# A short-convolution layer on one core: adaLN's weight loads on GpSimd's queue, paced by the other weights' splits

## The chip, the core and the metric

The kernel runs on one core of a Trainium2 chip. The metric is device time in microseconds (us), smaller is better. TensorE (PE in the profile) multiplies, VectorE (DVE), ScalarE (ACT) and GpSimd (POOL) compute beside it, and SyncE (SP) only starts DMA transfers. Each engine has a queue of instructions that it works through in order, and an instruction waits on semaphores for what it needs. A transfer is started by an instruction on some engine's queue, which waits there for its buffer to be free, and then runs on 16 DMA engines that all queues share.

## The reference

One layer of a decoder trunk (DEPTH is 1, so only the short-convolution mixer is used), for a sequence of 256 and a width of 2048, in float32:

```python
h = rmsnorm(x, norm_g[0])
mod = jnp.einsum('bd,df->bf', jax.nn.silu(c), ada_w) + ada_b     # adaLN: (2048) x (2048, 6144)
shift, scale, gate = jnp.split(mod, 3, axis=-1)
h = h * (1.0 + scale) + shift
proj = jnp.einsum('bsd,de->bse', h, w_in)                        # (256, 2048) x (2048, 16384)
b_gate, c_gate, v, g = jnp.split(proj, 4, axis=-1)
u = causal_depthwise_conv(c_gate * v, conv_w)
y = jnp.einsum('bse,ed->bsd', b_gate * u * silu(g), w_out)       # (256, 4096) x (4096, 2048)
out = rmsnorm(x + gate * y, final_g)
```

The weights are read once: `w_in` is 128 MB, `w_out` 32 MB, and adaLN's `ada_w` 48 MB, of which shift and scale take 32 MB and gate 16 MB. Shift and scale are needed before anything of `w_in` can be multiplied, row block by row block: row block k of h (128 of the 2048 rows, k from 0 to 15) needs 128 sums of shift and 128 of scale.

## The kernel before

**Float32 products by halves.** Each float32 weight tile `raw` is split into a rounded high part `hi` (a cast on ScalarE, line 324) and a low part `lo` (raw minus hi on VectorE, line 325), and so is h (`hT`). A product is three matmuls: hi by hi, hi by lo, lo by hi (line 417 to 419). `split` (lines 320 to 326) does this for one weight tile. The tiles `raw`, `hi` and `lo` have three buffers each. So the load of weight tile n waits for the low part of tile n-3, and the splits of tile n wait for TensorE to finish with tile n-3. The splits are counted here in the order in which the program makes them: 0 and 1 are in the front, 2 to 81 in the first main stage.

**The front** (lines 183 to 358) loads x, the vectors and the first 4 MB of adaLN for row blocks 0 and 1 (`first_ada`), sums these on VectorE and, in its last part, on TensorE (`sum0`, line 337; the call at line 351 is the last one), and makes row blocks 0 and 1 of `hT`. Its instructions are held in the order of the program.

**The first main stage** (mm_s, lines 444 to 502) works on half of `w_in`'s columns, in 16 sets (4 chunks by 4 quarters) of 512 columns. Since row blocks of h become ready only as adaLN's sums are done, each set is taken in several parts, first for the row blocks 0 and 1, later for more; what a part has summed is kept in `acc` and put back into the accumulator (`seed`). `part` (line 444) loads the weights in tiles of up to four row blocks (512 KB for two, 1 MB for four), splits each and multiplies.

**adaLN behind the front.** Row blocks 2 to 15 come in seven groups of two. A group is eight pieces (`ada_piece`, line 378): a piece loads, by two DMAs of 256 KB, two blocks of `ada_w`'s rows for shift and scale into a tile `at` (four buffers; the loads stand at line 388, on SP's queue), and sums them into `gv` by two VectorE operations of 512 elements (`ada_sums`, lines 394 to 401). After the eighth piece `ada_done` (line 403) adds up the partitions: TensorE transposes `gv` (`tp_g`, line 408), ScalarE sums the rows (line 410), and `modulate` (line 300) makes two row blocks of `hT`.

**What sets the order.** `plan` (line 52) is a planner with fixed costs: it lists parts and pieces in one order, in which a piece is put in wherever its load does not make the next weights late. The program is written down in this order, but a scheduler then orders each engine's queue by its own account of when each instruction can start; `later(300)` (line 168) makes an instruction 300 places less urgent, and `behind` and `add_manual_dep` with `after` are orders on one engine without a wait. So a load that needs only a free buffer can be put far ahead of its place in the plan. The planner's order puts the pieces ahead of the weights of these splits:

| row blocks | splits that the eight pieces stand ahead of | first needed by the weights of |
|---|---|---|
| 2, 3 | 4, 5, 7, 8, 9, 10, 12, 13 | 14 |
| 4, 5 | 14, 15, 16, 16, 17, 17, 19, 20 | 22 |
| 6, 7 | 21, 23, 23, 24, 24, 25, 26, 26 | 28 |
| 8, 9 | 27, 29, 29, 29, 31, 31, 33, 33 | 35 |
| 10, 11 | 34, 34, 36, 36, 38, 38, 38, 40 | 43 |
| 12, 13 | 40, 42, 42, 42, 44, 44, 46, 46 | 49 |
| 14, 15 | 46, 48, 48, 48, 50, 50, 50, 52 | 55 |

Splits 2 to 13 and 17 to 21 are of two row blocks, and so are some later ones (28, 30, 32 and others); most of the others are of four.

**Behind it** come the second half of `w_in` (mm_b, lines 545 to 581), with the loads and sums of adaLN's gate among it (`gate_piece`, line 520, and `gate_sums`, line 529: 32 loads of 512 KB into buffers of the same tag `at`), and then `w_out` (mm_o, lines 586 to 681).

Of the kernel before, what the change touches and what calls it, by code (L numbers as in the profile page):

```python
# [8 lines left out]
F32 = mybir.dt.float32  # L9
F32R = mybir.dt.float32r  # L10
AF = mybir.ActivationFunctionType
ALU = mybir.AluOpType

P = 128
# [3 lines left out]
KT = D // P  # L18
# [99 lines left out]
def short_conv_layer(ctx: ExitStack, tc: tile.TileContext, x, c, norm_g, ada_w, ada_b, w_in, conv_w, w_out, final_g, out):  # L118
    nc = tc.nc
# [19 lines left out]
    def raw_tile(name):  # L139
        return wpool.tile([P, SLOT], F32, tag="raw", name=name, bufs=3)  # L140

    after = mybir.DependencyInfo(mybir.DependencyClass.NoSync, mybir.DependencyReason.DATA)

    @contextmanager
    def in_order():
# [11 lines left out]
    @contextmanager  # L157
    def behind(last):

        traced = nc.cur_bb.bb.instructions  # L160
        n = len(traced)
        yield
        for ins in list(traced[n:]):
            if ins.engine in last:
                tc.add_manual_dep(ins, last[ins.engine], after, reason="behind")

    @contextmanager
    def later(n):

        now = tc.cur_priority  # L170
        tc.cur_priority = now + n
        yield
        tc.cur_priority = now
# [13 lines left out]
    GIVE = 300  # L187
# [12 lines left out]
    adas = ada_w[0].rearrange("(k p) (s f) -> p k s f", p=P, s=3)  # L200
# [18 lines left out]
    ones = const.tile([P, P], F32, tag="ones", name="ones")  # L219
# [38 lines left out]
    for t in range(TT):  # L258
        for dh in range(2):
# [3 lines left out]
            else:  # L263
                nc.vector.scalar_tensor_tensor(
                    out=junk[:, t], in0=xt[t][dh], scalar=1.0, in1=xt[t][dh], op0=ALU.mult, op1=ALU.mult,
# [54 lines left out]
    def split(raw, n, lo_tag="lo"):  # L320

        hi = wpool.tile([P, SLOT], F32R, tag="hi", name="hi", bufs=3)
        lo = wpool.tile([P, SLOT], F32R, tag=lo_tag, name="lo", bufs=3)
        nc.scalar.copy(hi[:, :n], raw[:, :n])  # L324
        nc.vector.tensor_tensor(out=lo[:, :n], in0=raw[:, :n], in1=hi[:, :n].bitcast(F32), op=ALU.subtract)  # L325
        return hi, lo


# [2 lines left out]
    gv0 = adap.tile([P, 2, 2 * P], F32, tag="gv", name="gv0")[:, :, 0 : NK0 * P]  # L331
    turn_x(0, 4)

    def sum0(k, rows, col):

        for o in range(2 * NK0):
            nc.tensor.matmul(
                sums0[:, o : o + 1], rows[:, o // NK0, (o % NK0) * P : (o % NK0 + 1) * P], col,
                start=k == ON_PE[0] and o == 0, stop=k is None, skip_group_check=True,
            )  # L340

    for k in range(KT):
        c_k = silu_c[:, k : k + 1]
# [4 lines left out]
            nc.vector.tensor_scalar_mul(gv0, first_ada[k], c_k)  # L348
        else:
            nc.vector.scalar_tensor_tensor(out=gv0, in0=first_ada[k], scalar=c_k, in1=gv0, op0=ALU.mult, op1=ALU.add)  # L350
    sum0(None, gv0, ones[:, 0:1])
    pieces0 = [split(raw0[:, 0 : CT * P], CT * P)]
    modulate(0, NK0, (sums0[:, 0:NK0], sums0[:, NK0 : 2 * NK0]))
    idle(IDLE[-1])
# [20 lines left out]
    acc = {}  # L375
    sums = {}

    def ada_piece(k0, nk, piece):
        w = nk * P
        kk = ASLOT // (2 * w)  # L380
        if piece == 0:
            sums[k0] = adap.tile([P, 2, 2 * P], F32, tag="gv", name="gv")
        gv = sums[k0][:, :, 0:w]
        j = piece * kk
        at = adap.tile([P, ASLOT], F32, tag="at", name="at", bufs=4)
        at4 = at.rearrange("p (k s f) -> p k s f", k=kk, s=2)
        for s in range(2):
            nc.sync.dma_start(at4[:, :, s, :], adas[:, j : j + kk, s, k0 * P : k0 * P + w])  # L388
        with later(GIVE):
            ada_sums(j, kk, at4, gv)  # L390
        if j + kk == KT:
            ada_done(k0, nk, gv)

    def ada_sums(j, kk, at4, gv):
        for i in range(kk):
            c_k = silu_c[:, j + i : j + i + 1]
            if j + i == 0:
                with behind(ended):
                    nc.vector.tensor_scalar_mul(gv, at4[:, i], c_k)
            else:  # L400
                nc.vector.scalar_tensor_tensor(out=gv, in0=at4[:, i], scalar=c_k, in1=gv, op0=ALU.mult, op1=ALU.add)  # L401

    def ada_done(k0, nk, gv):

        tp = psum.tile([P, 4, P], F32, tag="sm", name="tp_g", bufs=2)
        gs = const.tile([P, 4], F32, tag="gs", name="gs", bufs=2)
        for o in range(2 * nk):
            nc.tensor.transpose(tp[:, o, :], gv[:, o // nk, (o % nk) * P : (o % nk + 1) * P], ident)  # L408
        for o in range(2 * nk):
            nc.scalar.activation(tp[:, o, :], tp[:, o, :], AF.Copy, accum_out=gs[:, o : o + 1])  # L410
        modulate(k0, nk, (gs[:, 0:nk], gs[:, nk : 2 * nk]))
# [32 lines left out]
    def part(ch, q, k0, k1, seed):  # L444


        col = q * E + ch * CT * P
        step = SLOT // (CT * P)
        first = k0
        bank = psum.tile([P, CT, T], F32, tag="mm", name="mm_s")  # L450
        if seed:
            nc.scalar.copy(bank, acc[ch, q])
        if pieces0:
            for k in range(NK0):
                chunk_products(bank, *pieces0[k], 0, k, k0, k1, late=True)
            pieces0.clear()
            k0 = NK0
        for s0 in range(k0, k1, step):
            sk = min(step, k1 - s0)
            n = sk * CT * P  # L460
            raw = raw_tile("raw_s")
            nc.sync.dma_start(
                raw[:, :n].rearrange("p (k f) -> p k f", k=sk),
                w_in[0, s0 * P : (s0 + sk) * P, col : col + CT * P].rearrange("(k p) f -> p k f", p=P),
            )
            hi, lo = split(raw, n)
            for i in range(sk):
                chunk_products(bank, hi, lo, i * CT * P, s0 + i, k0, k1, seed)
        keep(ch, q, first, bank, seed)
# [57 lines left out]
            gate_sums(dc, j, at3)  # L527

    def gate_sums(dc, j, at3):
        nc.sync.dma_start(at3, adas[:, j : j + 2, 2, dc * 512 : (dc + 1) * 512])  # L530
        if j == 0:
            gacc[0] = adap.tile([P, 512], F32, tag="gv", name="gacc")
        ga = gacc[0]
        for i in range(2):
            s = silu_c[:, j + i : j + i + 1]
            if j + i == 0:
                nc.vector.tensor_scalar_mul(ga, at3[:, i, :], s)
            else:
                nc.vector.scalar_tensor_tensor(out=ga, in0=at3[:, i, :], scalar=s, in1=ga, op0=ALU.mult, op1=ALU.add)
        if j + 2 == KT:  # L540
            ps = psum.tile([P, 512], F32, tag="sm", name="ps_gate", bufs=2)
            nc.tensor.matmul(ps, ones, ga, start=True, stop=True)  # L542
            nc.vector.tensor_tensor(out=gate(dc), in0=ps, in1=gate(dc), op=ALU.add)
# [3 lines left out]
    for ct in range(NS, NCT, 2):  # L547
        for q in QUARTERS:
            bank = psum.tile([P, CT, T], F32, tag="mm", name="mm_b")[:, 0:2]
            col = q * E + ct * P  # L550
            for kp in range(0, KT, KP):
                raw = raw_tile("raw")
# [4 lines left out]
                hi, lo = split(raw, SLOT)  # L557
# [67 lines left out]
    for dc in range(4):  # L625
# [10 lines left out]
        for ep in range(n_ep):  # L636

            first = dc == 0 and ep == 0
            raw = wpool.tile([P, SLOT], F32, tag="raw" if first else "lo", name="raw_o", bufs=3)
# [4 lines left out]
            if dc == 3:  # L644
# [3 lines left out]
                    out=raw3, in0=raw3, in1=gate(dc).unsqueeze(1).to_broadcast([P, EP, 512]), op=ALU.mult  # L648
                )
            hi, lo = split(raw, SLOT, "raw")  # L650
# [55 lines left out]
```

## Time and profile before

| | |
|---|---|
| time, median of 3 runs | 925.6 us (924.58 to 927.4) |
| the profiled execution: span from its first to its last instruction | 925.9 us (no other time of its own is listed) |
| granted TensorE clock, mean | 0.995 |
| busy: PE, DVE, ACT, POOL | 904.4, 613.9, 472.8, 0.7 us |
| HBM | 224.49 MB read, 2.10 MB written |
| first matmul of the first main stage | at 26.5 us |
| mm_s to about 394 us, mm_b to about 743 us, then mm_o | |

The span of the profiled execution lies among the three run times, so it is taken as it stands. In the profile's lists a row of the timeline gives start, duration, engine, line, operation and the tiles (out<-in), and in brackets the idle time of the engine before it with what ended it; "x8" are instructions merged into one row. A row of the waits gives who waited for whom, the sum in us, how often, and the longest. A row of the windows gives for a stretch of time each engine's busy time with its count, the granted clock, the DMA share and GB/s. SPq is SP's queue, on which the DMAs are started.

### The profile page before, as it was taken

To read this page: it belongs to the slowest core of one execution; us is meant where nothing else is said; L and a number is where in the kernel's file an instruction comes from. 1 tells how busy PE (TensorE), PEld (TensorE's weight loads), DVE (VectorE), ACT (ScalarE), POOL (GpSimd) and SP (SyncE) were. 2 spreads that over 40 slices of the span, in tenths; PEclk is the share of its full clock that TensorE was granted. 3 is DMA by queue.
4 is the path that set the end of the run, shared out by engine and by line. 5 is a ranking of instruction groups with operands and counts; after the bars stand their busy time and mean duration, and the time that the engine had idled before them with its cause. 6 is when DMAs were issued, how large, how long until landed. Compare 5 with 4: busy or idle time off the path is not lost.

```text
span 925.9 us, 16464 instructions
## 1 busy us (share of the span) xinstructions
PE 904.4 (98%) x7119; PEld 869.6 (94%) x7119; DVE 613.9 (66%) x604; ACT 472.8 (51%) x465; POOL 0.7 (0%) x6
## 2 busy tenths in 40 slices
PE   7999899999999999999999999999999999999996
PEld 6999899999999999999999999999999988888885
DVE  5889888898486799875554455445554544545882
ACT  3787776675557856644434433443334433444333
POOL 0000000000000000000000000000000000000000
PEclk9999999999999999999999999999999999999999
DMA  9999999999895789776655665666556496566542
GB/s 314 355 367 355 367 329 338 350 365 358 268 306 186 219 297 357 243 231 201 202 186 188 199 204 184 189 199 204 183 183 195 140 348 226 186 200 205 182 137 92
DMA packets 163753, 227.66 MB, mean 246 GB/s; under 512 B 5680, under 2 KB 104160, under 8 KB 163296
## 3 DMA queue, kind: packets, MB, share of 16 engines
q1 hardware_dynamic: 163440, 226.51, 74.0%
q8 instruction: 56, 0.92, 0.4%
q14 instruction: 17, 0.14, 0.0%
q10 hardware_dynamic: 240, 0.09, 0.0%
HBM read 224.49 MB, written 2.10 MB: 245 GB/s over the span
## 4 chain that ended last, share of the span: by engine, by line
PE 88%; DMA 6%; DVE 3%; issue 1%; SPq 1%; ACT 1%; ACTq 0%; DVEq 0%
PE mm_b L419 38%; PE mm_s L419 31%; PE mm_o L604 6%; PE mm_o L605 6%; PE mm_o L603 6%; DMA at<-in_ada_w_dram 3%; DMA raw_s<-in_sc_w_in_dram 2%; DVE gv L401 1%; DVE lo L325 1%; DMA x<-in_x_dram 1%; SPq L212 0%; ACT hi L324 0%; PE ps_gate L542 0%; PE tp_g L408 0%; SPq L388 0%
## 5 line engine op out<-in xcount | busy, mean ns | idle before, releaser
L419 PE MATMUL mm_s<-hT,hi 128*128 128x256 f32 x2048 | 352.9, 278 | 0.1
L419 PE MATMUL mm_b<-hT,hi 128*128 128x256 f32 x2048 | 348.8, 276 | 0.0
L419 PEld LDWEIGHTS mm_s<-hT,hi 128*128 128x128 f32 x2048 | 310.4, 189 | 1.2 <-issue 0.5
L419 PEld LDWEIGHTS mm_b<-hT,hi 128*128 128x128 f32 x2048 | 308.4, 188 | 0.2 <-issue 0.2
L419 PE MATMUL mm_s<-hT,lo 128*128 128x256 f32 x1024 | 284.4, 279 | 6.8 <-DVE lo L325 6.7
L419 PE MATMUL mm_b<-hT,lo 128*128 128x256 f32 x1024 | 282.6, 276 | 0.0
L325 DVE TENSOR_TENSOR lo<-raw,hi 128x2048 fp32r<-128x2048 f32 (+1 forms) x66 | 148.1, 2244 | 135.1 <-ACT hi L324 135.1
L324 ACT CAST hi<-raw 128x2048 fp32r<-128x2048 f32 (+1 forms) x66 | 123.7, 1874 | 208.5 <-PE mm_b L419 150.2
L419 PEld LDWEIGHTS mm_s<-hT,lo 128*128 128x128 f32 x1024 | 193.1, 189 | 7.6 <-DVE lo L325 7.6
L419 PEld LDWEIGHTS mm_b<-hT,lo 128*128 128x128 f32 x1024 | 192.2, 188 | 0.2 <-issue 0.2
L325 DVE TENSOR_TENSOR lo<-raw_s,hi 128x2048 fp32r<-128x2048 f32 (+1 forms) x80 | 147.9, 1849 | 40.5 <-ACT hi L324 39.7
L324 ACT CAST hi<-raw_s 128x2048 fp32r<-128x2048 f32 (+1 forms) x80 | 124.6, 1557 | 67.6 <-PE mm_s L419 49.8
L325 DVE TENSOR_TENSOR lo<-raw_o,hi 128x2048 fp32r<-128x2048 f32 x32 | 73.3, 2291 | 65.1 <-ACT hi L324 65.0
L324 ACT CAST hi<-raw_o 128x2048 fp32r<-128x2048 f32 x32 | 61.0, 1907 | 107.2 <-PE mm_o L605 85.0
L604 PE MATMUL mm_o<-lo,y 128*128 128x512 f32 x256 | 99.7, 391 | 0.0
L603 PE MATMUL mm_o<-hi,y 128*128 128x512 f32 x256 | 99.3, 389 | 0.0
L605 PE MATMUL mm_o<-hi,y 128*128 128x512 f32 x256 | 99.3, 389 | 0.0
L401 DVE SCALAR_TENSOR_TENSOR gv<-at,silu_c,gv 128x512 f32<-128x512 f32 x105 | 78.6, 749 | 9.2 <-DMA at<-in_ada_w_dram 7.8
L440 ACT COPY acc<-mm_s 128x1024 f32<-128x1024 f32 x54 | 54.4, 1010 | 35.1 <-PE mm_s L419 34.9
L605 PEld LDWEIGHTS mm_o<-hi,y 128*128 128x128 f32 x256 | 48.0, 188 | 10.1 <-issue 0.2
L604 PEld LDWEIGHTS mm_o<-lo,y 128*128 128x128 f32 x256 | 48.0, 188 | 10.1 <-issue 0.2
L603 PEld LDWEIGHTS mm_o<-hi,y 128*128 128x128 f32 x256 | 48.0, 188 | 10.0
(94 smaller groups left out, 375.4 us busy)
## 6 DMA issues: line engine op xcount, KB each, us to landing
raw<-in_sc_w_in_dram SPq DMA_DIRECT2D x64, 1024.0 KB, 5.7
raw_s<-in_sc_w_in_dram SPq DMA_DIRECT2D x47, 1024.0 KB, 7.8
raw_o<-in_sc_w_out_dram SPq DMA_DIRECT2D x32, 1024.0 KB, 5.2
at<-in_ada_w_dram SPq DMA_DIRECT2D x114, 256.0 KB, 7.3
raw_s<-in_sc_w_in_dram SPq DMA_DIRECT2D x33, 512.0 KB, 5.8
at_g<-in_ada_w_dram SPq DMA_DIRECT2D x32, 512.0 KB, 8.0
at<-in_ada_w_dram SPq DMA_DIRECT2D x6, 512.0 KB, 8.8
x<-in_x_dram SPq DMA_DIRECT2D x4, 512.0 KB, 6.1
```

Of the source, the lines that this page charges most:

```text
L324: nc.scalar.copy(hi[:, :n], raw[:, :n])
L325: nc.vector.tensor_tensor(out=lo[:, :n], in0=raw[:, :n], in1=hi[:, :n].bitcast(F32), op=ALU.subtract)
L401: nc.vector.scalar_tensor_tensor(out=gv, in0=at4[:, i], scalar=c_k, in1=gv, op0=ALU.mult, op1=ALU.add)
L419: mm = last_mm[0] = nc.tensor.matmul(dst, w, h[:, k], start=begins and left, stop=ends, skip_group_check=True)
L440: nc.scalar.copy(acc[ch, q], bank)
L603: nc.tensor.matmul(po, yh, hi[:, o], start=opens, stop=False, skip_group_check=True)
L604: nc.tensor.matmul(po, yh, lo[:, o], start=False, stop=False, skip_group_check=True)
L605: nc.tensor.matmul(po, yl, hi[:, o], start=False, stop=ct == NCT - 1, skip_group_check=True)
```

## The change

Four things are changed; no arithmetic is.

1. The loads of the pieces behind the front (112 DMAs) and of the gate (32 DMAs) are started from GpSimd's queue, not from SP's.
2. Each load of a piece waits, by a semaphore, for the low part of the split three before the next one (`splits[n - 3]`, where n is the number of splits made so far), or, for the first one, for the last of the front's sums on TensorE. The gate's loads get no such wait.
3. A piece's sums (and after the eighth, `ada_done`) are written down later: after the split of the weights that follow the piece in the plan, and on VectorE they are put behind that split's low part (an order, without a wait).
4. `split` and `sum0` give out the instructions that this needs.

```diff
+    done = mybir.DependencyInfo(mybir.DependencyClass.Sync, mybir.DependencyReason.DATA)
+    splits = []
...
-        nc.vector.tensor_tensor(out=lo[:, :n], in0=raw[:, :n], in1=hi[:, :n].bitcast(F32), op=ALU.subtract)
+        lo_op = nc.vector.tensor_tensor(out=lo[:, :n], in0=raw[:, :n], in1=hi[:, :n].bitcast(F32), op=ALU.subtract)
+        splits.append(lo_op.ins)
...
-    sum0(None, gv0, ones[:, 0:1])
+    front_sums = sum0(None, gv0, ones[:, 0:1])
...
+    waiting = []
+
+    def summed():
+
+        while waiting and waiting[0][0] < len(splits):
+            n, todo = waiting.pop(0)
+            with behind({mybir.EngineType.DVE: splits[n].name}):
+                todo()
...
+        n = len(splits)
         for s in range(2):
-            nc.sync.dma_start(at4[:, :, s, :], adas[:, j : j + kk, s, k0 * P : k0 * P + w])
-        with later(GIVE):
-            ada_sums(j, kk, at4, gv)
-        if j + kk == KT:
-            ada_done(k0, nk, gv)
+            load = nc.gpsimd.dma_start(at4[:, :, s, :], adas[:, j : j + kk, s, k0 * P : k0 * P + w])
+            tc.add_manual_dep(load.ins, splits[n - 3].name if n > 4 else front_sums.name, done, reason="in turn with the weights")
+
+        def sums_of():
+            with later(GIVE):
+                ada_sums(j, kk, at4, gv)
+            if j + kk == KT:
+                ada_done(k0, nk, gv)
+
+        waiting.append((n, sums_of))
...
             hi, lo = split(raw, n)
+            summed()
...
-        nc.sync.dma_start(at3, adas[:, j : j + 2, 2, dc * 512 : (dc + 1) * 512])
+        nc.gpsimd.dma_start(at3, adas[:, j : j + 2, 2, dc * 512 : (dc + 1) * 512])
```

3 lines of the change are left out of this document (2 added, 1 removed).

## The prediction, made before the run

> **What bounds the kernel now.** I read the page first, its busy shares and its chain of work that ended last.
>
> ```profile
> span 925.9 us, 16464 instructions
> PE 904.4 (98%) x7119; PEld 869.6 (94%) x7119; DVE 613.9 (66%) x604; ACT 472.8 (51%) x465; POOL 0.7 (0%) x6
> ...
> PE 88%; DMA 6%; DVE 3%; issue 1%; SPq 1%; ACT 1%; ACTq 0%; DVEq 0%
> ```
>
> TensorE is the bound. The same chain in order of time says from when on:
>
> ```profile
> 92.42 0.37 SPq L388
> 92.84 9.18 DMA at<-in_ada_w_dram
> 102.10 0.76 DVE gv L401
> ...
> 103.55 2.30 DVE lo L325
> 105.89 23.69 PE mm_s L419 x192
> 129.69 13.66 PE mm_s L419 x120
> ```
>
> From 105.89 us on the chain stays on PE, at 13.66 / 120 = 0.1138 us a matmul; nothing in the change makes a matmul cheaper, so all that can be won lies ahead of it. The windows and the waits of that stretch:
>
> ```profile
> 30.00:110.00 80.00, 73.16 (x620) 72.14 (x620) 72.61 (x94) 62.50 (x85) 0.00 (x0) 0.98 1.07 362
> 110.00:230.00 120.00, 120.00 (x1056) 120.00 (x1055) 103.86 (x124) 80.00 (x90) 0.00 (x0) 1.00 1.02 349
> ```
> ```profile
> PE mm_s L419 <- DVE lo L325: 6.7, 3, 3.7
> DVE gv L401 <- DMA at<-in_ada_w_dram: 5.5, 6, 2.2
> ```
>
> From 30 to 110 us PE is busy 73.16 of 80 us; from 110 on it has no gap. Three waits for a low part make 6.7 us. The timeline of PE shows the three, and what follows the last:
>
> ```profile
> 34.68 0.39 PE L419 MATMUL mm_s<-hT,lo 128*128 128x256 f32 x1 [1.09 <-DVE lo L325]
> ...
> 71.05 0.39 PE L419 MATMUL mm_s<-hT,lo 128*128 128x256 f32 x1 [1.91 <-DVE lo L325]
> ...
> 105.89 0.39 PE L419 MATMUL mm_s<-hT,lo 128*128 128x256 f32 x1 [3.69 <-DVE lo L325]
> ...
> 107.47 0.42 PE L419 MATMUL mm_s<-hT,lo 128*128 128x256 f32 x1
> ...
> 110.04 0.41 PE L419 MATMUL mm_s<-hT,lo 128*128 128x256 f32 x1
> ```
>
> After 107.47 three matmuls take (110.04 - 107.47) / 4 = 0.64 us, not 3 x 0.1138 = 0.34: a slower clock after the longest wait. It lasts five such periods, 5 x 0.30 = 1.5 us. So 6.7 + 1.5 = **8.2 us** can be won, and what is left is PE's own work.
>
> Why is the low part late? VectorE and ScalarE around the three places (splits 3, 14 and 22):
>
> ```profile
> 30.38 3.11 DVE L401 SCALAR_TENSOR_TENSOR gv<-at,silu_c,gv 128x512 f32<-128x512 f32 x4
> 33.41 1.22 DVE L325 TENSOR_TENSOR lo<-raw_s,hi 128x1024 fp32r<-128x1024 f32 x1
> ```
> ```profile
> 68.05 0.75 DVE L401 SCALAR_TENSOR_TENSOR gv<-at,silu_c,gv 128x512 f32<-128x512 f32 x1 [1.33 <-DMA at<-in_ada_w_dram]
> 68.71 2.28 DVE L325 TENSOR_TENSOR lo<-raw_s,hi 128x2048 fp32r<-128x2048 f32 x1
> ```
> ```profile
> 102.10 1.54 DVE L401 SCALAR_TENSOR_TENSOR gv<-at,silu_c,gv 128x512 f32<-128x512 f32 x2 [2.22 <-DMA at<-in_ada_w_dram]
> 103.55 2.28 DVE L325 TENSOR_TENSOR lo<-raw_s,hi 128x2048 fp32r<-128x2048 f32 x1
> ```
> ```profile
> 31.99 1.04 ACT L324 CAST hi<-raw_s 128x1024 fp32r<-128x1024 f32 x1
> ...
> 66.67 1.92 ACT L324 CAST hi<-raw_s 128x2048 fp32r<-128x2048 f32 x1
> ...
> 99.10 1.91 ACT L324 CAST hi<-raw_s 128x2048 fp32r<-128x2048 f32 x1
> ```
>
> The high part of split 22 is done at 101.01, but VectorE stands until 102.10 before a sum whose load has not landed, and takes up the low part at 103.55: 2.5 us of the 3.69 are that order. Split 14 is different: its high part ends at 68.59 and the low part starts at 68.71, so it was the weights that came late. Split 3 waits for its high part until 33.03, which ScalarE did late; VectorE adds 0.4.
>
> For the splits 14 and 22, the starts of their loads on SP's queue, the DMA issues of the window from 21 to 57.3 us, and adaLN's loads in the view of the tile `at`:
>
> ```profile
> 57.35 0.37 SPq L462 DMA_DIRECT2D raw_s<-in_sc_w_in_dram  x1
> ...
> 90.97 0.37 SPq L462 DMA_DIRECT2D raw_s<-in_sc_w_in_dram  x1
> ```
> ```profile
> at<-in_ada_w_dram SPq DMA_DIRECT2D x30, 256.0 KB, 6.6
> ```
> ```profile
> L388 SPq DMA_DIRECT2D at<-in_ada_w_dram x112: 367/460/3009, 21.9 to 190.9; - x112
> ...
> DMA to landing us min/median/max: 4.7/7.4/11.4
> ```
>
> Split 14's load was started at 57.35 and its cast at 66.67, 9.3 us later, for 1 MB that by 362 GB/s takes 2.9 us: the rest is queue, and much of the queue is adaLN. By 57.3 us 30 loads, 15 pieces, were out, and all 112 by 190.9. The planner's order has the last piece ahead of split 52, whose pace in the change is split 49, the low part at 230.05 in
>
> ```profile
> 230.05 2.29 DVE L325 TENSOR_TENSOR lo<-raw_s,hi 128x2048 fp32r<-128x2048 f32 x1
> ```
>
> So adaLN runs up to 40 us ahead of need, in the stretch where DMA is full.
>
> **The change part by part.** *Pacing.* What must be loaded fits PE's time if it comes in the planner's order. From split 14 to 26 PE has 42 row blocks x 12 matmuls x 0.1138 = 57.4 us of work; the weights are 42 x 256 KB and the 16 pieces ahead of splits 15 to 27 are 8 MB, together 19.4 MB (of 10^6), by 362 GB/s 53.6 us. From 27 to 47 it is 95.6 us of work against 17.5 + 12 MB = 30.9 x 10^6 bytes, 85.4 us. So with the loads in turn split 14's 9.3 us of queue shrink: against the 15 pieces, the pace allows 9 by then (those ahead of splits 4 to 14), so 3 MB or 8.7 us less go ahead of it. It was late by 1.91: that wait goes, and what is late next is ScalarE's cast, with nothing ahead of it.
>
> *Sums behind the next low part.* At split 22 the sums no longer stand ahead: 2.5 us directly, and the remaining 1.2 of 3.69 by the earlier landing (8.1 us from 90.97 to 99.10). With the wait goes the slow clock, 1.5. At split 3 only VectorE's 0.4 goes; the 0.7 that ScalarE makes stays.
>
> Won: 1.9 + 3.7 + 1.5 + 0.4 = **7.5 us**.
>
> *GpSimd's queue.* It takes over 112 + 32 starts. GpSimd starts no DMA in this trace; the nearest row is SP's start at line 388, 0.37 to 3.0 us, median 0.46, and those bound it. I take 0.46, the row's own median, but the sum needs less: 16 pieces are 32 starts in 57.4 us, 1.8 us each, the next 24 pieces 48 starts in 95.6 us, 2.0. Below 1.8 it is hidden behind PE, and nothing else stands on that queue except later pieces and the gate; above, it is the second rival. SP loses as many starts (112 x 0.46 = 52 us of its queue), worth nothing alone: its wait is for the low parts, not for time.
>
> *The added waits.* A piece now starts when the low part three splits back is done, which is when the weights of the next split get their buffer too. It then has three splits (8 us of PE's time for two row blocks, 16 for four) until its sums may run; landing took 7.4, at most 11.4. That fits with four row blocks, and just with two. Behind a waiting load stand only later loads; VectorE waits for them where they are late. The new order costs: a group's last sums, 1.5 us, end that much after a low part, and TensorE's transposes of `gv` stand in its queue. Seven groups; I charge **1.0 us** in all, bounded by 0 and by 7 x 1.5 = 10.5. Around 28 us, where four pieces ran ahead before, DMA will have less to do; that costs nothing, as the weights' own loads there wait for buffers.
>
> *The gate's loads* on GpSimd's queue come behind adaLN's; mm_b has no PE gap to win or lose.
>
> Sum: 925.9 - 7.5 + 1.0 = **919.4 us**, made against the profiled span; the runs' median, 925.6, lies 0.3 below it, too little to shift it for.
>
> *A page that speaks against it.* VectorE's rows in the stretch are these, by the groups of instructions:
>
> ```profile
> L325 DVE TENSOR_TENSOR lo<-raw_s,hi 128x2048 fp32r<-128x2048 f32 (+1 forms) x80 | 147.9, 1849 | 40.5 <-ACT hi L324 39.7
> L399 DVE TENSOR_SCALAR gv<-at,silu_c 128x512 f32<-128x512 f32 x7 | 3.4, 483 | 0.1
> ```
>
> The Trainium skill, "SBUF — State Buffer", § SBUF: two separate sides, warns that a DMA from GpSimd's queue has its descriptors written by GpSimd's cores, which are locked out while VectorE runs an operation in a two-port mode. Its § Who interferes with whom says that tensor_tensor has no such mode and tensor_scalar can have one; by that a start here waits at most one short operation, and the sum stays. Were the lock held by every VectorE operation, a start would wait up to the low part's 2.28 us, above the 1.8 that decides: that is the second rival below.
>
> **The rivals.** *Only the order on VectorE counts* (the weights come no sooner, since DMA is full at 362 GB/s either way): 2.5 + 1.5 + 0.4 are won, 1.0 lost, **922.5**. For it: DMA's share is 1.07 through the stretch. Against: the bytes needed fit the time with 7 to 10% to spare.
>
> *GpSimd's starts are slow* (slower than before). Over 1.8 us a start, groups 4 to 15 come late by 32 + 48 starts times the excess. At 2.2 us: 32 x 0.4 + 48 x 0.2 = 22 us, less about 8 us that a group is ahead of its need (row blocks 4 and 5: from split 20 to 22, three parts of two row blocks, 3 x 24 x 0.1138), less the 7.5 won: +6.5 to +7, **932.5**. For it: no row shows this queue; SP's own worst start took 3.0. Against: SP's median.
>
> *TensorE stands at the transposes* (slower, or no gain): up to 10.5 lost, against 7.5 won: from 918.4 to **928.9**. It decides if a low part ends less than the sums' 1.5 us ahead of PE. Against it, the waits from 110 to 394 us:
>
> ```profile
> ACT hi L324 <- PE mm_s L419: 52.2, 31, 4.4
> ```
>
> ScalarE waits for PE to free buffers, so the low parts are then ahead of PE by most of a split. Before 75 us they were not.
>
> *The gate's loads run ahead* (they have no pace): 16.8 MB by 362 GB/s are 46 us of DMA in the full stretch; a third of it, 15 us, makes 925.9 - 7.5 + 15 = **933**. Against:
>
> ```profile
> L530 SPq DMA_DIRECT2D at_g<-in_ada_w_dram x32: 367/368/773, 193.4 to 368.9; - x32
> ```
>
> They began at 193.4, after the last piece at 190.9, though nothing but a buffer holds them back: buffers of a tag seem to be given in the program's order.
>
> **How the numbers follow.** The forecast, 916 to 922: 0.58. Only the order: 0.15, half of it under 922.8. Transposes, 922 to 929: 0.10, mostly no change or slower. Slow starts: 0.12. Gate ahead: 0.05. A measurement of this kernel tells 0.3% (2.8 us) from no change. Faster: 0.58 + 0.07 = 0.65. Within 0.3%: 0.08 + 0.04 = 0.12. Slower: 0.12 + 0.05 + 0.06 = 0.23. Range: all 8.2 won and nothing lost is 917.7; 916 leaves 1.7 below it, about what the lowest run (924.58) lies below the span. At the top 931 takes in the transposes' whole bound and starts of up to nearly 2.2 us.
>
> **What would show it.** Right: no wait of PE for `lo` at splits 14 and 22, no slow clock near 100 us, PE busy near 79 of 80 us from 30 to 110; adaLN's loads on GpSimd until about 225 us; the waits of VectorE for `at` nearly gone. Wrong: PE waiting for `gv` or `hT` (transposes, or slow starts, told apart by GpSimd's busy time a start, against 1.8 us); weights that land no sooner than 8 us after their start with DMA full (order only); loads of `at_g` ahead of 190 us (gate ahead).

## The result, and the profile after

The changed kernel takes **947.1 us** (median of 4 runs, 946.2 to 948.9) against 925.1 us for the kernel before on the same chip: ratio 1.0239, 95% interval 1.0219 to 1.0260. It is 22 us slower; 919.4 was forecast. The profiled execution has a span of 945.0 us. Its page, with the busy line of TensorE, the shares of the chain that ended last, and the row of GB/s by fortieths of the span:

```profile
span 945.0 us, 16467 instructions
...
PE 912.5 (97%) x7119; PEld 875.5 (93%) x7119; DVE 613.6 (65%) x604; ACT 471.9 (50%) x465; POOL 104.9 (11%) x150
...
GB/s 314 269 333 228 337 237 264 331 290 355 362 344 326 289 299 358 231 220 224 188 191 205 185 193 206 182 194 206 180 196 192 147 322 235 203 181 200 199 134 89
...
PE 80%; DMA 11%; ACT 3%; DVE 2%; issue 2%; ACTq 0%; SPq 0%; DVEq 0%
```

DMA's share of the chain went from 6 to 11%, and the transfers no longer fill the engines: the second to seventh fortieth (24 to 165 us) swing between 228 and 337 GB/s. Where the time goes is best read by counting matmuls in windows. First the kernel before, then the changed one; the number in the first brackets is how many PE instructions started in the stretch, the fractions near the end are the granted clock and DMA's share:

```profile
24.00:60.00 36.00, 34.89 (x290) 34.28 (x290) 32.90 (x47) 27.23 (x35) 0.00 (x0) 0.95 1.06 360
60.00:100.00 40.00, 37.94 (x327) 37.31 (x326) 36.86 (x52) 31.06 (x46) 0.00 (x0) 1.00 1.06 360
100.00:150.00 50.00, 46.31 (x393) 46.12 (x392) 40.86 (x47) 36.40 (x45) 0.00 (x0) 0.97 1.02 343
150.00:200.00 50.00, 50.00 (x443) 50.00 (x442) 44.83 (x61) 35.52 (x47) 0.00 (x0) 1.00 1.03 348
200.00:250.00 50.00, 50.00 (x443) 50.00 (x442) 35.45 (x30) 28.03 (x19) 0.00 (x0) 1.00 0.93 329
```
```profile
24.00:60.00 36.00, 35.04 (x293) 34.45 (x293) 25.96 (x35) 26.86 (x34) 13.98 (x20) 0.95 0.86 282
60.00:100.00 40.00, 36.05 (x285) 34.87 (x283) 27.81 (x35) 23.52 (x31) 12.13 (x17) 0.91 0.83 278
100.00:150.00 50.00, 40.82 (x314) 39.39 (x315) 31.72 (x41) 33.45 (x45) 15.91 (x23) 0.93 0.87 288
150.00:200.00 50.00, 48.79 (x429) 48.59 (x428) 37.42 (x42) 30.36 (x34) 17.20 (x24) 1.00 0.88 287
200.00:250.00 50.00, 47.46 (x406) 47.27 (x405) 42.89 (x51) 31.23 (x40) 20.37 (x29) 0.97 1.01 347
```

The changed kernel is 3 matmuls ahead at 60 us, then loses 42, 79, 14 and 37: 169 in all from 24 to 250 us. At 50 / 443 = 0.113 us each that is 19.1 us, which is the whole difference of the spans (945.0 - 925.9). The medians lie 22 apart: a time is 1.8 us above its span here (946.76 and 945.0), so the profiled execution of the kernel before was one of its slower ones. So the loss lies between 60 and 250 us, seven tenths of it before 150. TensorE's busy time from 60 to 250 us fell from 184.25 to 173.12 us, so 11.1 us are waits; the other 8 are mostly the clock (0.91, 0.93 and 0.97 in windows where the kernel before had 1.00, 0.97 and 1.00). The gate and all that follows cost nothing (from 250 to 390 us both kernels start 1226).

The waits of the changed kernel (who waited for whom: us, times, longest):

```profile
POOL at L402 <- DVE gv L420: 87.1, 25, 10.9
...
ACT hi L326 <- PE mm_s L438: 73.2, 33, 7.6
...
ACT hi L326 <- DMA raw_s<-in_sc_w_in_dram: 45.3, 21, 5.2
POOL at L402 <- DVE lo L327: 33.3, 13, 6.1
...
PE mm_s L438 <- ACT mm_s L471: 7.4, 5, 3.2
...
PE mm_s L438 <- DVE lo L327: 5.1, 6, 1.2
```

TensorE's 6.7 us before low parts became 5.1, and the 3.69 at split 22 are gone: that part of the forecast came. New are waits for the seed copies (L471), and ScalarE waits 45.3 us for weights (13.9 before). The seed copies stand in ScalarE's queue behind casts that wait.

The first loss, near 70 us, is at split 14, whose weights come as late as before. These are the start of its load, its cast, and its first two waits on TensorE:

```profile
57.01 0.37 SPq L481 DMA_DIRECT2D raw_s<-in_sc_w_in_dram  x1
```
```profile
66.97 1.90 ACT L326 CAST hi<-raw_s 128x2048 fp32r<-128x2048 f32 x1 [4.40 <-DMA raw_s<-in_sc_w_in_dram]
...
69.83 0.65 PE L438 MATMUL mm_s<-hT,hi 128*128 128x256 f32 x2 [2.04 <-ACT acc L459]
71.25 0.58 PE L438 MATMUL mm_s<-hT,lo 128*128 128x256 f32 x1 [0.77 <-DVE lo L327]
```

From there to 76.86 us three matmuls take 0.64 us in place of 0.34. The larger loss comes after it. ScalarE's timeline shows how that begins; the row blocks' modulation is line 316 (hT), the casts line 326:

```profile
78.44 1.09 ACT L316 ACTIVATE hT<-xs,shift,scale 128x256 fp32r<-128x256 f32 x2
87.14 1.05 ACT L326 CAST hi<-raw_s 128x1024 fp32r<-128x1024 f32 x1 [7.60 <-PE mm_s L438]
...
109.91 1.91 ACT L326 CAST hi<-raw_s 128x2048 fp32r<-128x2048 f32 x1 [2.61 <-DMA raw_s<-in_sc_w_in_dram]
...
115.78 1.90 ACT L326 CAST hi<-raw_s 128x2048 fp32r<-128x2048 f32 x1 [1.86 <-DMA raw_s<-in_sc_w_in_dram]
...
121.56 1.10 ACT L316 ACTIVATE hT<-xs,shift,scale 128x256 fp32r<-128x256 f32 x2 [2.40 <-DVE scale L312]
```

In the kernel before the same two rows of hT, for row blocks 2, 3 and 4, 5, are these:

```profile
68.48 1.09 ACT L314 ACTIVATE hT<-xs,shift,scale 128x256 fp32r<-128x256 f32 x2
...
83.07 1.09 ACT L314 ACTIVATE hT<-xs,shift,scale 128x256 fp32r<-128x256 f32 x2 [1.55 <-DVE scale L310]
```

Row blocks 2, 3 come 10 us later and 4, 5 come 38.5 us later. Their use is fixed by the plan: the second half of split 14 needs 2, 3, and that of split 22 needs 4, 5. In the kernel before those halves began at 73.67 and 109.6 us, so the slack, counted from the start of hT, was 5 and 27 us. For row blocks 2, 3 even that is too much: the low parts of hT, which VectorE makes after it, were ready at 74.04 us, less than 2 us ahead of their own use; in the changed kernel they were ready at 83.52. First the kernel before, then the changed one:

```profile
73.62 0.42 DVE L318 TENSOR_TENSOR hT<-xs,hT 128x256 fp32r<-128x256 f32 x1
```
```profile
82.76 0.76 DVE L320 TENSOR_TENSOR hT<-xs,hT 128x256 fp32r<-128x256 f32 x2
```

The change ate 10 and 38. The program's order on TensorE, set when it is built, shows the consequence. For splits 14 to 18 it is, as split:matmuls,

```
before   14:48 15:48 16:48 17:24 18:24
changed  14:24 15:24 16:2 14:1 15:1 16:23 14:12 15:7 14:11 15:16 16:23 18:24 17:24
```

(four transposes that stand inside split 14 are left out). First halves are run while second halves wait for their row blocks, so three splits hold all three weight buffers at once. The cast at 87.14, of split 17, stands 7.6 us for the buffer of split 14, whose last product starts at 86.94; the loads behind it start late, and TensorE meets them late.

### The profile page after: what moved, and what is told of

Its sections match the earlier page's. It is cut to its first block, busy times and chain, and to the rows that moved or that the text cites. A ratio compares the mean times of both kernels' runs of the same rounds, so it can differ in the third digit from the quotient of the medians.

```text
span 945.0 us, 16467 instructions
## 1 busy us (share of the span) xinstructions
PE 912.5 (97%) x7119; PEld 875.5 (93%) x7119; DVE 613.6 (65%) x604; ACT 471.9 (50%) x465; POOL 104.9 (11%) x150
## 3 DMA queue, kind: packets, MB, share of 16 engines
q0 software_dynamic: 13568, 46.15, 14.0%
## 4 chain that ended last, share of the span: by engine, by line
PE 80%; DMA 11%; ACT 3%; DVE 2%; issue 2%; ACTq 0%; SPq 0%; DVEq 0%
PE mm_b L438 37%; PE mm_s L438 24%; DMA raw_s<-in_sc_w_in_dram 9%; PE mm_o L623 6%; PE mm_o L625 6%; PE mm_o L624 6%; ACT hi L326 2%; DMA at<-in_ada_w_dram 2%; DVE lo L327 1%; DVE gv L420 1%; DMA x<-in_x_dram 1%; ACT acc L459 0%; PE ps_gate L562 0%; PE sum L340 0%; ACT x L291 0%
## 5 line engine op out<-in xcount | busy, mean ns | idle before, releaser
L438 PE MATMUL mm_s<-hT,hi 128*128 128x256 f32 x2048 | 359.2, 281 | 12.6 <-ACT mm_s L471 7.4
L438 PEld LDWEIGHTS mm_s<-hT,hi 128*128 128x128 f32 x2048 | 315.1, 192 | 15.1 <-ACT mm_s L471 8.4
L438 PEld LDWEIGHTS mm_s<-hT,lo 128*128 128x128 f32 x1024 | 195.3, 191 | 7.3 <-DVE lo L327 7.0
L402 POOL DMA_DIRECT2D at<-in_ada_w_dram x112 | 81.0, 725 | 171.4 <-DVE gv L420 87.1
```

What stands on the lines that cost most here:

```text
L402: load = nc.gpsimd.dma_start(at4[:, :, s, :], adas[:, j : j + kk, s, k0 * P : k0 * P + w])
L438: mm = last_mm[0] = nc.tensor.matmul(dst, w, h[:, k], start=begins and left, stop=ends, skip_group_check=True)
```

## The experiments

Theory 1: two queues share the 16 DMA engines, pieces started later overtake weights, and the weights land late. Theory 2: the pace starts the pieces too late. Theory 3: the sums behind the next low part hold the four buffers. After four runs a fourth was formed: **row blocks late**, whichever part makes them so. All times (each ratio is to the kernel before run beside it, 924.4 to 925.7 us), with the start of hT for row blocks 2, 3 / 4, 5 / 14, 15 and the median us from start to landing of a 1 MB raw_s load, from each run's profile (before: 68 / 83 / 261 and 7.8):

| kernel | us | ratio to before (95%) | hT at | raw_s |
|---|---|---|---|---|
| changed (queue, pace, sums) | 947.1 | 1.0239 (1.0219 to 1.0260) | 78 / 122 / 280 | 8.5 |
| e1_sync (pace, sums) | 937.2 | 1.0139 (1.0113 to 1.0165) | 77 / 116 / 273 | 7.8 |
| e2_no_pace (queue, sums) | 945.3 | 1.0226 (1.0186 to 1.0267) | 83 / 124 / 280 | 8.3 |
| e3_sums_before (queue, pace) | 951.4 | 1.0295 (1.0270 to 1.0321) | 82 / 127 / 288 | 8.5 |
| e4_sums_only | 933.6 | 1.0100 (1.0078 to 1.0122) | 77 / 115 / 267 | 8.0 |
| e5_queue_only | 939.0 | 1.0155 (1.0139 to 1.0171) | 79 / 119 / 273 | 9.1 |
| e6_pace_only | 952.1 | 1.0292 (1.0277 to 1.0307) | 82 / 121 / 288 | 8.4 |
| e8_in_order | 951.9 | 1.0302 (1.0274 to 1.0331) | 81 / 127 / 283 | 8.7 |
| e15_early1 | 943.2 | 1.0194 (1.0150 to 1.0239) | 81 / 122 / 266 | 9.3 |
| e16_early2 | 940.2 | 1.0154 (1.0127 to 1.0181) | 80 / 112 / 251 | 9.1 |
| e7_early3 | 932.6 | 1.0073 (1.0039 to 1.0108) | 68 / 105 / 241 | 9.6 |
| e12_no_pace_early3 | 932.6 | 1.0080 (1.0062 to 1.0098) | 67 / 105 / 237 | 8.8 |
| e17_gate_back | 929.2 | 1.0048 (1.0024 to 1.0071) | 68 / 103 / 237 | 8.6 |
| e10_one_queue_early3 | 925.4 | 1.0006 (0.9997 to 1.0015) | 67 / 104 / 229 | 7.5 |
| e18_one_queue_early4 | 924.6 | 0.9990 (0.9978 to 1.0001) | 62 / 88 / 225 | 7.8 |
| e9_sums_early3 | 927.5 | 1.0026 (1.0013 to 1.0038) | 64 / 99 / 226 | 8.0 |
| e13_one_software_queue | 932.4 | 1.0075 (1.0049 to 1.0101) | 71 / 110 / 234 | 8.2 |
| e14_swapped_queues | 940.0 | 1.0150 (1.0123 to 1.0177) | 69 / 107 / 239 | 8.7 |
| e11_before_late1 | 932.8 | 1.0078 (1.0058 to 1.0098) | 69 / 84 / 269 | 7.8 |

### The three parts, one by one

**One queue again.** Against the changed kernel:

```diff
-            load = nc.gpsimd.dma_start(
+            load = nc.sync.dma_start(
...
-        nc.gpsimd.dma_start(at3,
+        nc.sync.dma_start(at3,
```

> The changed kernel, with adaLN's loads and the gate's loads issued by SyncE again, in the weights' queue; the pace and the later sums stay. Theory 1 (two queues share the 16 engines, and a piece started later takes bandwidth from weights started earlier, which land 10 to 15 us after their start instead of 7 to 10): in one queue the order of starting is the order of landing, the waits of ScalarE's casts for raw_s fall back from 45 us toward the 13.9 us of the kernel before, and the time is 917 to 927 us. Theory 2 (the pace starts the pieces too late, the engines idle early and are late afterwards): the pace is still there, so the DMA row keeps its holes and the time stays at 940 us or more. Theory 3 (the sums behind the next low part hold the four at buffers and make the row blocks late): also 940 us or more, with waits of the loads for gv of some 80 us, now in SyncE's queue.

937.2 us: 9 of the 22 us come back, and raw_s lands in 7.8 us as before, but ScalarE still waits 32.3 us for it and the row blocks are nearly as late (77 and 116 us). Neither theory 1 nor theory 2 alone.

**No pace.**

```diff
-            tc.add_manual_dep(load.ins, splits[n - 3].name if n > 4 else front_sums.name, done, ...)
+            tc.add_manual_dep(load.ins, front_sums.name, done, ...)
```

> The changed kernel without the pace: every piece's load waits only for the sums of the front (and for its at buffer), still on GpSimd; the later sums stay. Theory 2 (the pace is the loss): the pieces run ahead as the buffers come free, DMA moves 340 GB/s or more from 20 to 60 us again, and the time is 930 us or less. Theory 1 (sharing between two queues): the weights still land 10 us and more after their start where pieces run beside them; 940 to 950 us. Theory 3: the buffers are still freed late; GpSimd's wait for gv rises from 87 us to 110 us or more, since the 33 us of the pace go over to it, and the time stays within 5 us of 947.

945.3 us, with an interval that overlaps the changed kernel's. With the sums where the change puts them the pace hardly matters: the pieces do not run ahead without it either, for GpSimd's waits for the sums' buffers rise from 87.1 to 115.6 us, as theory 3 said.

**Sums as before.** The sums are called right behind the load and `waiting` stays empty.

```diff
-        def sums_of():
-            with later(GIVE):
-                ada_sums(j, kk, at4, gv)
-            if j + kk == KT:
-                ada_done(k0, nk, gv)
-
-        waiting.append((n, sums_of))
+        with later(GIVE):
+            ada_sums(j, kk, at4, gv)
+        if j + kk == KT:
+            ada_done(k0, nk, gv)
```

> The changed kernel with a piece's sums written right behind its load, as in the kernel before, and not behind the next low part; the loads stay on GpSimd and paced. Theory 3 (the later sums hold the buffers): GpSimd's waits for gv fall from 87 us to under 40 us, and the time is 930 us or less. Theories 1 and 2: the weights land as late as in the changed kernel, ScalarE's casts wait 35 us or more for raw_s, and the time stays between 940 and 955 us.

951.4 us: GpSimd now waits for the pace (106.9 us for lo) in place of the buffers, and VectorE stands 32.3 us before sums whose loads are late. So theory 3 alone falls too.

**Only the sums' new place.** The first diff's loads on SyncE, and no added wait.

> The kernel before with only the sums' new place (behind the next weights' low part); loads on SyncE, no pace. Theory 3: the loss comes with the sums, 940 us or more. Theories 1 and 2: the sums' place is harmless; VectorE no longer waits for at ahead of a low part, so PE's waits for lo (3.7 us at 114 us and 1.9 us at 71 us in the kernel before) shrink and the time is 918 to 926 us.

933.6 us, 9.2 slower, between both forecasts. (The wait of 3.7 us in the kernel before stands at 105.89 us, not at 114.) VectorE waits for `at` only 1.9 us in its accumulating sums (L419) and TensorE 2.6 us for lo, both as hoped; and yet it is slower:

```profile
PE mm_s L437 <- ACT mm_s L470: 5.0, 2, 3.2
```
```profile
77.24 1.10 ACT L316 ACTIVATE hT<-xs,shift,scale 128x256 fp32r<-128x256 f32 x2 [2.88 <-DVE scale L312]
84.23 1.05 ACT L326 CAST hi<-raw_s 128x1024 fp32r<-128x1024 f32 x1 [5.89 <-PE mm_s L437]
```

One queue, no pace, and the same signs as in the changed kernel: hT 9 us late, splits 14 to 16 interleaved in TensorE's order, the cast at 84.23 waiting 5.9 us for a buffer. This run is where theory 4 was formed.

**Only the queue**, from the kernel before, with the sums as before and a wait for the front's sums alone.

> The kernel before with only the queue changed: adaLN's and the gate's loads on GpSimd, behind the sums of the front, no pace, sums where they were. Theory 1 (two queues share the engines, weights land late): nearly the whole loss comes with the queue, 940 us or more, and the weights of splits 14 to 16 and 22 to 25 land 10 us and more after their start. Theory 4 (formed after the first four runs: each part of the change makes adaLN's row blocks later; TensorE's program then runs the first halves of three splits ahead of their second halves, which holds all three weight buffers, and the loads behind them stop): what counts is when the row blocks are ready. Here they are tied to no split, so the loss is less than in the changed kernel, 928 to 940 us, and goes with how late the second row blocks' hT is against the 83 us of the kernel before.

939.0 us, 14.1 slower, inside theory 4's range and 1 us under theory 1's 940, which its interval reaches; so the time alone does not decide. Both signs are there: row blocks 4, 5 come at 119 instead of 83 us, and raw_s lands in 9.1 instead of 7.8 us.

**Only the pace**, on SyncE, sums as before.

> The kernel before with only the pace: adaLN's loads stay in SyncE's queue, but each waits for the low part three splits back; sums where they were. Theory 1: one queue, so no overtaking, within 5 us of the kernel before (920 to 930 us). Theory 2 (the pace starts pieces too late) and theory 4: the row blocks come later by the loads' waiting (the second ones' hT at 90 us or later instead of 83 us), splits 14 to 16 are interleaved on TensorE, and the time is 930 to 940 us.

952.1 us: the pace alone costs 27.2 us, more than forecast by any theory. The waits:

```profile
ACT hi L326 <- DMA raw_s<-in_sc_w_in_dram: 77.1, 29, 8.2
...
DVE gv L417 <- DMA at<-in_ada_w_dram: 37.0, 19, 4.3
...
PE mm_s L435 <- DVE lo L327: 18.7, 9, 3.8
```

The piece comes late, VectorE stands 37.0 us before its sums with the next low part behind them, and TensorE waits 18.7 us for low parts. The sums' new place takes most of that wait away (e1: 4.9 us) and gives some 15 us back. So the pace alone costs by late low parts as well as by late row blocks (hT at 82 and 121 us). The parts alone cost 14.1 + 27.2 + 9.2 = 50.5 us, together 22.0: they do not add, since each delays the same row blocks and one takes away a wait that another makes.

### Is it the lateness, or the order on TensorE?

**In order.** The changed kernel, each split's products behind the last of the split before:

```diff
-            for i in range(sk):
-                chunk_products(bank, hi, lo, i * CT * P, s0 + i, k0, k1, seed)
+            with behind({mybir.EngineType.PE: last_mm[0].ins.name}):
+                for i in range(sk):
+                    chunk_products(bank, hi, lo, i * CT * P, s0 + i, k0, k1, seed)
```

> The changed kernel with TensorE's matmuls kept in the order of the splits: each split's products stand behind the last product of the split before. Theory 4 has two readings. Reading a (the interleaving is the loss, since it holds three splits' buffers at once): buffers come free in turn, the loads run ahead, and the time falls to 925 to 935 us. Reading b (the late row blocks are the loss, and the interleaving only hid a part of it): TensorE now waits for hT in the middle of split 14, some 6 to 10 us near 73 us, and again in split 22, and the time is 945 to 965 us. Theory 1: order alone changes little, 940 to 950 us, with late weights.

951.9 us, reading b: the interleaving only hid a part. TensorE's timeline now has the waits for the row blocks in plain sight:

```profile
81.17 0.40 PE L438 MATMUL mm_s<-hT,hi 128*128 128x256 f32 x1 [3.92 <-ACT hT L316]
...
85.30 0.58 PE L438 MATMUL mm_s<-hT,hi 128*128 128x256 f32 x1 [3.74 <-DVE hT L320]
```
```profile
127.76 0.58 PE L438 MATMUL mm_s<-hT,hi 128*128 128x256 f32 x1 [8.88 <-ACT hT L316]
```

That is 7.7 us for row blocks 2, 3 and 8.9 for 4, 5, in the middle of splits 14 and 22.

**Pieces earlier.** The plan's list is reordered at its end, three weight parts forward; e15 and e16 have 1 and 2 for 3, e18 has 4:

```diff
-    return steps
+    parts, moved = 0, []
+    for step in steps:
+        moved.append((max(0, parts - 3) if step[0] == "ada" else parts, step[0] == "mm", len(moved), step))
+        parts += step[0] == "mm"
+    return [step for _, _, _, step in sorted(moved)]
```

> The changed kernel with every adaLN piece put three weight parts earlier in the written order; queue, pace and the sums' rule stay. Theory 4: the row blocks are ready as early as in the kernel before or earlier (second ones' hT at 95 us or sooner instead of 121 us), TensorE's program keeps splits 14 to 16 and 22 to 24 in order, the casts no longer wait 7 us for buffers at 80 us, and the time is 930 us or less. Theory 1: the two queues share the engines just the same, weights land as late, 940 us or more.

932.6 us: 14 of the 22 us are back with queue, pace and sums as in the change. Row blocks 2, 3 and 4, 5 come at 67.7 and 105.2 us, before their use, splits 14 to 16 are in order, and ScalarE's longest wait for TensorE there is 3.8 instead of 7.6 us. The 930 forecast was missed by 2.6.

> The changed kernel with the pieces one weight part earlier. Theory 4: the time falls with each part, from 947 us (none) to 932.6 us (three), here 940 to 945 us, with the second row blocks' hT some 4 to 8 us sooner than at 121.6 us. If only the order of splits 14 to 16 and 22 to 24 on TensorE counts, which is still interleaved here, the time stays at 944 to 949 us.

> The changed kernel with the pieces two weight parts earlier. Theory 4, step by step: 935 to 940 us. Splits 22 to 24 are in order here and 14 to 16 still are not, so if the order alone counts about half of the 14.3 us comes back, 938 to 942 us.

0, 1, 2, 3 parts give 947.1, 943.2, 940.2, 932.6 us, falling with each step, though the interval of one part overlaps those of none and of two. At one part row blocks 2, 3 and 4, 5 are no sooner (81 and 122), against what was expected; only the later ones are (266 instead of 280). Whether those count by themselves is not shown. At two parts splits 22 to 24 are in order and 14 to 16 are not, and 940.2 fits the order's range as well as, at its edge, the steps'. Lateness and interleaving move together here, and e8 is what tells them apart.

**The kernel before, made late.** The same edit with `parts + 1` in the kernel before.

> The kernel before with nothing changed but the written order: every adaLN piece one weight part later. One queue, no pace, sums behind their loads. Theory 4: lateness alone costs, for each part is 3 to 6 us of TensorE's work, and the kernel before has no slack at splits 14 and 22 (TensorE waited there for lo, and the row blocks came within 3 us of their use): 930 to 945 us. Theory 1: no second queue, no loss, 922 to 928 us.

932.8 us, in the range of theory 4, but the loads start as before (21.3 to 163.9 us for the seven groups' first ones, 21.9 to 167.0 before), and only the last row blocks came later, 269 for 261 us; TensorE waits 3.4 us for a seed copy at 319. It tells nothing of row blocks 2 to 5, which came at 69 and 84 us as before. (The expectation puts the row blocks within 3 us of their use; that holds for 2, 3, while 4, 5 had 27 us.)

**One queue, three and four parts earlier.**

> The changed kernel with the pieces three parts earlier, and the loads of adaLN and of the gate on SyncE: against the same kernel with GpSimd's queue (932.6 us) this is the price of the queue when the row blocks are in time. Theory 1 in its weaker form (sharing costs some us through weights that land 10 us and more after their start): 920 to 928 us, with the raw_s landings at 7 to 9 us. Theory 4 alone (only row blocks count): the same 930 to 935 us.

925.4 us: with pace and sums as in the change, but one queue and the pieces early, the whole loss is gone. Against e7 the queue costs some 7 us. The landing rows of e7, then of e10 (KB each, median us):

```profile
raw_s<-in_sc_w_in_dram SPq DMA_DIRECT2D x47, 1024.0 KB, 9.6
...
at<-in_ada_w_dram POOLq DMA_DIRECT2D x112, 256.0 KB, 6.7
```
```profile
raw_s<-in_sc_w_in_dram SPq DMA_DIRECT2D x47, 1024.0 KB, 7.5
...
at<-in_ada_w_dram SPq DMA_DIRECT2D x114, 256.0 KB, 6.9
```

and ScalarE's waits for weights, again e7 and e10:

```profile
ACT hi L330 <- DMA raw_s<-in_sc_w_in_dram: 51.7, 24, 5.8
```
```profile
ACT hi L330 <- DMA raw_s<-in_sc_w_in_dram: 11.1, 10, 1.9
```

So a weaker theory 1 stands beside theory 4: on a second queue the pieces land as fast and the weights 2.1 us later.

The gain that was forecast does not come even here. Two windows of e10:

```profile
24.00:60.00 36.00, 33.14 (x270) 32.02 (x270) 26.04 (x36) 24.83 (x31) 0.00 (x0) 0.95 0.89 294
...
100.00:150.00 50.00, 49.02 (x429) 48.62 (x429) 47.26 (x61) 40.35 (x52) 0.00 (x0) 1.00 1.06 363
```

From 100 to 150 us it starts 36 matmuls more than the kernel before (429 for 393; the wait for the low part at split 22 is 0.92 us in place of 3.69), but from 24 to 60 us 20 fewer (270 for 290), where DMA moved 294 GB/s for 360.

> The changed kernel with the pieces four weight parts earlier, and adaLN's and the gate's loads on SyncE. Theory 4 (lateness): with three parts the row blocks are in time already, so a fourth wins nothing more, 923 to 929 us; a gain under 922 us would say that row blocks still bound that kernel, a loss over 930 us that the earlier loads now hold up the weights.

924.6 us, no difference from the kernel before that can be told. Row blocks at 62 and 88 us win nothing more; of all the versions none is faster than the kernel before.

**Without one of the parts, three parts earlier.**

> The kernel before with the sums' new place (behind the next low part) and every adaLN piece written three weight parts earlier; loads on SyncE, no pace. With the sums' new place alone the time was 933.6 us and the second row blocks' hT came at 115 us. Theory 4 (late row blocks are the loss): earlier pieces make the row blocks early again, TensorE's order is straight, and VectorE's low parts no longer stand behind sums that wait for at: 915 to 925 us. Theory 3 (the sums behind the low parts cost by themselves, by holding buffers and filling VectorE): 930 to 935 us as without the shift.

927.5 us, just above theory 4's range and well under theory 3's. The sums behind the low parts cost 2.3 us (0.13 to 0.38%) once the row blocks are in time, instead of 9.2.

> The changed kernel without the pace and with the pieces three parts earlier (loads on GpSimd, sums behind the next low part). If the pace costs more than lateness, this beats the paced one (932.6 us): 918 to 928 us. If the queue's sharing is what is left, the loads start sooner and overtake more weights, and the time is 930 to 940 us.

932.6 us, the same as with the pace: the pace costs nothing any more, and what is left is the queue.

### What in the queue costs 7 us

> The changed kernel with the pieces three parts earlier and only the gate's loads back on SyncE; adaLN's stay on GpSimd. If the queue's price (7 us) comes from adaLN's pieces beside the first stage's weights, nothing changes: 930 to 935 us. If it comes from the gate's loads, 924 to 928 us.

929.2 us, between both ranges. The intervals of e17 and e10 lie apart, so adaLN's loads alone cost some 4 us on GpSimd's queue; those of e7 and e17 overlap, so the gate's share, some 3 us, is not sure.

The weights' issue in `part()` on GpSimd too (e13), or instead (e14, from e10):

```diff
-            nc.sync.dma_start(
+            nc.gpsimd.dma_start(
                 raw[:, :n].rearrange("p (k f) -> p k f", k=sk),
```

> The changed kernel with the pieces three parts earlier, and the weights raw_s of the first stage on GpSimd as well: one queue for adaLN and the weights, but GpSimd's. If the price of the queue (932.6 against 925.4 us) is that there are two of them and the pieces overtake the weights, it goes: 923 to 929 us, with raw_s landing 8 us or less after its start. If it is GpSimd's way of loading, it stays or grows: 931 us or more.

932.4 us, in the range of "GpSimd's way of loading", though raw_s lands in 8.2 us, nearer to one queue's 7.5. But 2.3 us of it arise before the first product, which starts at 29.3 us for 26.9 in e7: the first weights now run beside the front's loads on SyncE (its 512 KB loads of at land in 10.9 us for 8.7). What stays is 930.

> The same with the queues exchanged: the weights raw_s on GpSimd, adaLN's and the gate's loads on SyncE, pieces three parts earlier. Two queues again. If the queues share packet by packet, the one with the larger packets (GpSimd's of 3.4 KB on average against 1 KB for adaLN's on SyncE) gets the larger part: raw_s lands sooner than in the kernel with adaLN on GpSimd (7 to 8 us instead of 9.6 us for 1 MB), at later (8 us or more instead of 6.7 us), and the time is 922 to 929 us. If any second queue costs the same, 930 to 936 us.

940.0 us, outside both ranges. The shares moved in the expected sense, raw_s 8.7 for 9.6 and `at` 7.6 for 6.7 us, but less than forecast. Some 3 us arise before the first product here too (at 29.8 for 26.9 us), and waits for low parts of 1.8, 1.3 and 1.2 us at 215, 262 and 295 us, of which e7 has only the first (1.6 at 220), cover the answer. Why GpSimd's queue costs 7 us is left open between sharing and the kind of queue.

## Why the prediction was wrong, point by point

- **The bound** was read rightly for the kernel before: TensorE's own work, with three waits for lo. In the changed kernel those at splits 14 and 22 shrank from 1.91 and 3.69 us to 0.77 and none, though at split 14 a wait of 2.04 for the copy of acc (L459), behind a cast that waited for weights, stands just ahead. "From 105.89 us on the chain stays on PE" is true of the kernel before and was carried over to the changed one; of the 169 lost matmuls 51 and part of the 79 lie behind that point.
- **The step that failed is the pacing:** "So adaLN runs up to 40 us ahead of need" and "That fits with four row blocks, and just with two". Need was taken as a piece's place in the plan, and a piece's time as landing before its sums. What TensorE needs is the row block, eight pieces, sums, transposes and modulation later, and its slack was 5 us or less for blocks 2, 3 and 27 us for 4, 5. The run-ahead was that slack. The step even counted it, 15 pieces out by 57.3 us against 9 (8 in the trace of the changed kernel), and called it queue. The pace alone, charged nothing, measured +27.2 us. In the changed kernel it is not the only brake, for without it (e2) the time is 945.3: the sums' new place holds the pieces back as well.
- **"8.7 us less go ahead of it ... that wait goes":** the pace's gain at split 14 did not come either. With 8 pieces out in place of 15 the split's load started at 57.01 us, and its cast at 66.97: 10.0 us after it, 9.3 before. On one queue with the same pace (e1) it was 7.7 us, so a part of the 10.0 seems to come with the second queue; the term of 1.9 us took the queue's length for the whole cause.
- **"Around 28 us ... DMA will have less to do; that costs nothing"** failed with it: 282 for 360 GB/s from 24 to 60 us is work missing later.
- **The new order, charged 1.0 us, bounded by 10.5:** the sums' new place alone measured +9.2, near the bound. The mechanism was not the one named (each group's last sums 1.5 us later): row blocks 2, 3 and 4, 5 came at 77 and 115 us. That buffers come free only at the pace of the splits is plainest in e2, where GpSimd waits 115.6 us for them. The prediction's own sign, PE waiting for hT, is what e8 shows; the program's order hides most of it in the changed kernel.
- **GpSimd's starts:** taken at 0.46, decisive at 1.8; measured, in the view of the tile `at`:

```profile
L402 POOL DMA_DIRECT2D at<-in_ada_w_dram x112: 724/724/841, 25.7 to 253.0; - x112
```

  That rival falls. The Trainium skill, "SBUF — State Buffer", § Who interferes with whom, says that tensor_tensor has no two-port mode and contends only with GpSimd's reads. The trace is in keeping with it: no start took longer than 0.84 us beside low parts of 2.3 us. That GpSimd's queue costs 7 us with the row blocks in time, and weights that land later, was no term and no rival. The Trainium skill, "DMA: Bandwidth & Descriptors", § Queues, rings and completion order, says that each DMA engine takes turns between queues packet by packet; the landing rows of e7 and e10 are in keeping with that, and it should have been a rival.
- **Gate ahead:** rightly refused; its loads began at 256.5, after adaLN's last at 253.0.
- **TensorE at the transposes** named a slower outcome, but its price, 928.9 at most, and its place were too small, and the range ended at 931.

## What to carry to other kernels

A load that runs far ahead in a full queue may be the slack of a long chain behind it: before pacing it, follow it to its last consumer (here row blocks, not sums) and compare ready time with use. When the engine that bounds a kernel shows no wait for a late operand, look at its program's order: it may run other work instead, and pay in buffers held. Parts that delay the same thing do not add, so price each alone and all together.

## What the runs showed of the hardware

Two rows of the changed kernel's queues (packets, MB, share):

```profile
q1 hardware_dynamic: 124272, 180.37, 58.7%
q0 software_dynamic: 13568, 46.15, 14.0%
```

GpSimd's queue moves 46.15 MB / 13568 = 3.4 KB a packet, SyncE's 1.45 KB, though the pieces' rows are the same 1 KB on either. A start of a 256 KB load by GpSimd takes 0.72 us with almost no spread, SyncE's 0.37 to 3.0. And TensorE's granted clock fell to 0.91 and 0.93 in stretches of 40 and 50 us in which no wait was longer than 3.3 us; after waits of 2.04 and 0.77 us three matmuls took 0.64 in place of 0.34 us, for some 7 us.
